# A recurrent chain's readouts: two kinds of products side by side, or one kind after the other

## The chip, the cores and the metric

The kernel runs on one core of one Trainium2 chip. The metric is device time in microseconds (us) from start to end of one execution; the median of several runs is quoted. PE is TensorE (products; PEld its weight loads), DVE is VectorE, ACT is ScalarE, POOL is GpSimd and SP the engine whose queue issues the DMAs.

## The reference

Two layers of a transformer block over 512 latent tokens (x) and 256 context tokens (ctx), width 1024. Each layer is an FFN, a mixing stage and a second FFN. The mixing stage has four mixers, one of which is RWKV-7, a linear recurrence run in both directions over the tokens, for four heads of 64 features:

```python
def wkv7_scan(r, decay, k, v, kk, b, s0, reverse):
    def step(s, inp):
        r_t, w_t, k_t, v_t, kk_t, b_t = inp
        sa = jnp.einsum('bhvk,bhk->bhv', s, kk_t)
        s = s * w_t[:, :, None, :] - sa[..., None] * b_t[:, :, None, :] + v_t[..., None] * k_t[:, :, None, :]
        return s, jnp.einsum('bhvk,bhk->bhv', s, r_t)     # state, readout
```

The second value of each step is the readout. The context's outputs aren't needed in the last layer, so that there the context's recurrence is run for its final state alone.

## The kernel before

Everything is laid out features first and written as generators of pieces of work. The program is a plain list of operations; a planner puts them into an order for each engine, from priorities and from the times that it works out for them, and adds the waits. PE runs its own list in that order.

The recurrence (`rwkv`) is computed in chunks of 64 tokens. A unit is two neighbouring chunks in one direction; the stages of successive units run beside each other: element-wise products and Gram matrices (`rw_elem`), inverses of small blocks by substitution on POOL (`rw_sub`, lines 1176 and 1177), inverses of whole chunks (`rw_lev`, lines 1203 to 1239), and the chain of states (`rw_chain`). Other work shares the engines: the first FFN of x while the context of layer 0 is in this stage, the second FFN of the context while x of layer 0 is, and attention and the RG-LRU mixer (lines 861 to 953) while x of layer 1 is. The FFNs' products, and all other products of large weights, stand on line 503.

In `rw_chain` each chunk has one bank of PSUM, the tile `pc`, in four parts of 128 columns: `pw`, `pu`, `ps` and `py`. The four heads lie as two pairs `p`; the two heads of a pair lie on partitions 0 to 63 and 64 to 127 (`H`). For each chunk there are

- line 1260: four products into `pw`, over 128 rows with 64 columns of weights; ACT copies them to `w` (line 1262)
- line 1266: four products into `pu`, over 64 rows with 64 columns of weights; ACT puts them into `uv` (line 1269)
- line 1275: four products into `ps`, over 128 rows: what the chunk adds to the state
- lines 1278 and 1279, only where the readout is needed: four products of the state over 128 rows into `py`, and four products of the chunk's own values over 64 rows that add to them
- line 1282: DVE makes the next state from `ps`, four operations; then line 1287 (ACT) or 1289 (DVE) brings `py` to `yt`

A product of float32 operands is two instructions on PE. All of `pc` is one bank, and the planner's waits keep the products into a bank and the reads of it in the order of the program, whichever parts they touch. The readout is needed for four context chunks of layer 0 in two directions (8), and for eight chunks of x in two directions in each layer (16 and 16): 40 chunks.

Of the kernel before, what the change touches and what calls it, by code (L numbers as in the profile page):

```python
# [15 lines left out]
D = 1024  # L16
# [12 lines left out]
# DRAM layout of eight [64, 64] matrices: the 16 x 16 blocks on all their diagonals lie one stride apart  # L29
MS = 4 * (BL * 64 + BL)  # L30

# columns of the packed shape constants
# [20 lines left out]
def shape_constants():  # L53
    import numpy as np

    c = np.zeros((128, C_N), np.float32)
    p = np.arange(128)
    c[p, C_ID + p] = 1.0
    s = p[:, None] % 64
    t = np.arange(64)[None, :]  # L60
    for d in range(2):
        strict = (s < t) if d == 0 else (s > t)
        incl = (s <= t) if d == 0 else (s >= t)
        for ty, m in enumerate((strict, incl)):
            o = C_MO + d * 128 + ty * 64
            c[:, o:o + 64] = m
        # mask for E[t, j]: row t in the later half, column j in the earlier half
        rows = (s // BL) % 2 == (1 if d == 0 else 0)
        cols = (t // BL) % 2 == (0 if d == 0 else 1)
        o = C_ML + d * 64  # L70
        c[:, o:o + 64] = rows & cols & (s // (2 * BL) == t // (2 * BL))
    c[:, C_I16:C_I16 + 256] = np.eye(16, dtype=np.float32).reshape(1, 256)
    c[:, C_RS:C_RS + 256] = np.arange(256)[None, :] % 64 != 0
    n = np.arange(NX, dtype=np.int32)
    inv = (np.float32(10000.0) ** (-np.arange(8, dtype=np.float32) / np.float32(8))).astype(np.float32)
    ang = np.stack([(n // 64).astype(np.float32)[:, None] * inv, (n % 64).astype(np.float32)[:, None] * inv], axis=1)
    ang = np.concatenate([ang, ang], axis=-1).reshape(NX, 32).astype(np.float32)
    for o in (0, 64):
        c[o:o + 32, C_RP:C_RP + 512] = np.cos(ang).astype(np.float32).T
        c[o + 32:o + 64, C_RP:C_RP + 512] = np.sin(ang).astype(np.float32).T  # L80
    return c


def arrange(inp):
    """the arrays as the launch takes them: tiles of weights contiguous, features first, small vectors as columns"""
# [38 lines left out]
def dhalf(t, h):  # L124
    """of eight [64, 64] matrices in DRAM every second one, from h on, as [64, 4, 64]"""
    return bass.AP(tensor=t.tensor, offset=t.offset + h * MS, ap=[[64, 64], [2 * MS, 4], [1, 64]])


def ddiag(t):
    """the 16 x 16 blocks on their diagonals as [32, 16, 16]"""  # L130
    return bass.AP(tensor=t.tensor, offset=t.offset, ap=[[MS // 4, 32], [64, BL], [1, BL]])


def upto(g, blocks):
    """the pieces of g up to the end of a number of its blocks"""
# [7 lines left out]
def some(g, n):  # L143
    """n pieces of g at a time"""
# [6 lines left out]
def merge(*gens):  # L151
    """the pieces of several generators in turn"""
# [5 lines left out]
def seg(t, s):  # L158
    """columns of t [p, 512]: s = 0, the middle half; 1, the outer quarters; None, all"""
# [3 lines left out]
def like(t, s):  # L163
    """t [p, 256] in the shape of such columns"""
# [15 lines left out]
class Net:  # L180
    def __init__(self, ctx, tc, ins, out):
# [4 lines left out]
        # the vector engine has much else to do while x goes through w_in: the low parts of its weights are GpSimd's  # L186
# [13 lines left out]
        # wb: a bank kept for the first stage of RWKV; piece: the last load of the modulations' weights  # L200
# [12 lines left out]
    def hold(self, name, side="left"):  # L213
        """a pool that stays until it is dropped"""
# [7 lines left out]
    def weights(self, side="left", raw=3, hi=2, lo=2):  # L222
        """the pool of the large weights"""
# [7 lines left out]
    def pM(self, h=None):  # L231
        """for the mixers: a bank for each of two of RWKV's stages (h), or for the others in turn"""
# [15 lines left out]
    # ---------------------------------------------------------------- setup  # L248
    def setup(self):
# [25 lines left out]
        # what the context leaves for the latent tokens of the same layer  # L275
# [34 lines left out]
    def params(self, l):  # L310
# [23 lines left out]
        # halves of the biases that go into tanh forms of sigmoids  # L334
# [9 lines left out]
        # softplus(-lambda)  # L344
# [15 lines left out]
    def ada(self, l):  # L360
        """mod[128, 72, 2]: feature chunk i * 8 + c of modulation i, for x and for ctx. Yields between pieces,
        True after each block of columns."""
# [39 lines left out]
    # ---------------------------------------------------------------- helpers  # L402
# [6 lines left out]
    def root(self, r, sums, n, eps):  # L409
        """r = 1 / sqrt(sums / n + eps)"""  # L410
# [7 lines left out]
    def rstd(self, tiles, N, groups, n, eps, tag="r", h=None):  # L418
        """1 / sqrt(sums / n + eps) of the sums of tiles over groups of partitions, on those partitions.
        The sums lie tokens first, a few columns, until they are spread"""  # L420
# [5 lines left out]
        # one accumulation: its start leaves none of the columns written, so that the first product for each replaces  # L426
# [11 lines left out]
    def meansq(self, pool, S, s, bank=None):  # L438
        """1 / rms of each token of a segment, on all partitions"""
# [16 lines left out]
    def norm(self, pool, hs, l, i, S, bank=None):  # L456
        """hs = modulated norm of the tokens, a segment at a time"""
# [15 lines left out]
    def loadw(self, src, new=None):  # L473
        """[128, nk, ncol] in DRAM -> exact high and low parts; new: where the tiles come from"""
# [22 lines left out]
    def gemm(self, W, c0, m, hs, N, ps=None, s=None, first=True, last=True):  # L497
        """PSUM tile [m, N] = W[:, :, c0:c0+m]^T hs, each operand a sum of two parts; s: only these columns"""
# [7 lines left out]
    def gemms(self, Ws, hs, S):  # L506
        """the products of several weights, a segment of the tokens after the other"""
# [16 lines left out]
    # ---------------------------------------------------------------- FFN  # L524
    @contextmanager
    def hidden(self, S, side="left"):
        """the tiles of an FFN: pools, input"""
# [7 lines left out]
    def ffn_groups(self, l, w13, w2, i, S, f, between=None, after=iter(())):  # L535
        """between: a generator of other pieces of work, one of which follows each tile of the hidden units;
        after: one that uses each segment of the result"""
# [31 lines left out]
    # ---------------------------------------------------------------- mixers  # L569
    def frame(self, S, a):  # L570
        """the mixers' inputs"""
# [14 lines left out]
    def mix(self, l, S, out, f=None, hs=None):  # L586
        """f: the tiles that hold the input, where nothing else wants the chip, so that the mixers run beside each other"""
# [49 lines left out]
    def others(self, l, S, out, pr, side, keep, first=iter(())):  # L637
        """first: the next of it comes before w_out; keep: the stack of pools that holds the tiles of w_out's rows"""
        if self.wide:
            # what is left of the modulations fills the tensor engine's gaps  # L640
# [45 lines left out]
    def wout(self, l, parts, S, s=None):  # L686
        """x += gate * (mixers' outputs @ their rows of w_out)"""
# [10 lines left out]
    def projector(self, l, S, hs, wp, nw=5, nr=2):  # L698
        """a tile of h @ w_in; work tiles of two kinds"""
# [5 lines left out]
    def winproj_c(self, l, S, hs, wp, out, pr):  # L705
# [6 lines left out]
        # C: token shift  # L712
# [18 lines left out]
        # normalised key  # L731
# [9 lines left out]
    def winproj(self, l, S, hs, wp, out, pr, nw=5, nr=2):  # L741
# [4 lines left out]
        # A: value times (1 + tanh(gate / 2)); the half is in the taps  # L746
# [9 lines left out]
        # D  # L756
# [30 lines left out]
        # B  # L787
# [11 lines left out]
        for c in range(2 if out else 0):  # L799
            ps = proj(768 + c * 128)  # L800
            # gelu, tanh form
# [10 lines left out]
    def rotcols(self, w):  # L812
        """columns 32..63 of w [128, k, 64] = the rotated partners of columns 0..31"""
# [5 lines left out]
    # ---- conv module  # L819
# [28 lines left out]
    # ---- RG-LRU  # L848
# [36 lines left out]
    # ---- MLA  # L885
    def mla(self, l, S, wp, yp, out, pr):
# [11 lines left out]
        # values, token-major  # L898
# [62 lines left out]
    # ---- RWKV-7  # L961
    def rwkv(self, l, S, wp, out, pr, deep):
        """stages of successive units run beside each other: element-wise products and Gram matrices; inverses of
        the blocks on the diagonals; inverses of the whole; chain of the states"""
# [34 lines left out]
    def rwkv_out(self, l, S, wp, pr, rw):  # L999
# [10 lines left out]
        for s in S.segs:  # L1010
            # the middle half is done while the last units are on their way, in the places of those that are through
# [31 lines left out]
    def slot(self, u, shape, tag, bufs):  # L1043
        """a tile in a ring of its own kind, each place of which lies where its first use puts it"""
        return u.wp.tile(shape, F32, tag=f"{tag}{u.i % bufs}", name=self.nm(tag), bufs=1)

    def rw_elem(self, u):
        """one direction of chunks b, b + 1 of all heads: 4 blocks q = 2 * pair + chunk, each with
        two heads on the diagonal"""
# [27 lines left out]
        # log of the decay products from a chunk's start, inclusive (cs) and exclusive (lw)  # L1077
# [17 lines left out]
        # channel-major: beta on the diagonal, kappa off it; alpha and rho on the diagonal, zeros off it  # L1095
# [37 lines left out]
        # token-major beta, kappa, scaled to the chunk's end  # L1133
# [20 lines left out]
    def gates(self, u, half):  # L1154
        """tanh forms of decay and rate of a direction's next four chunks"""
# [9 lines left out]
    def rw_sub(self, u):  # L1165
        """-(1 + L)^-1, transposed, of the 16 x 16 blocks on the diagonals by substitution, a block to a partition"""
# [25 lines left out]
    def rw_lev(self, u):  # L1192
        """the same of whole chunks by doubling blocks"""
# [3 lines left out]
        # values, token-major, off the diagonal (head 0 on partitions 64.., head 1 on partitions 0..)  # L1197
# [15 lines left out]
        def each(f):  # L1213
            """[128, 4, 64] in PSUM: f of each matrix's part and partitions"""
# [12 lines left out]
        # the last level has one block of 32 x 32 to fill, rows B, columns A  # L1227
# [14 lines left out]
    def rw_chain(self, u):  # L1242
# [11 lines left out]
        for c in order:  # L1254
# [19 lines left out]
            for p, H in PH if more else []:  # L1274
                nc.tensor.matmul(ps[H, p * 64:p * 64 + 64], bk[:, p * 2 + c, H], uv[:, p, H], start=True, stop=True)
            for p, H in PH if need_y else []:
                o, q = py[H, p * 64:p * 64 + 64], p * 2 + c
                nc.tensor.matmul(o, sv[:, p, H], wr[:, q, 1, H], start=True, stop=False)  # L1278
                nc.tensor.matmul(o, uv[H, p, H], lq[H, q, 1, :], start=False, stop=True)  # L1279
# [12 lines left out]
    # ---------------------------------------------------------------- end  # L1292
# [123 lines left out]
```

## Time and profile before

| | |
|---|---|
| median of 3 runs | 3439.17 us (3435.9 to 3445.69) |
| span of the profiled execution | 3440.0 us |
| PE busy | 3255.4 us (95% of the span) |
| DVE, ACT, POOL busy | 2020.9, 1389.9, 961.0 us |
| chunks with a readout | 40, in the stretches 713 to 846 us (8), 1408 to 1626 us (16), 2798 to 2970 us (16) |

The profiled execution took as long as the runs did. A product written as 128*64 in a row has 128 rows and 64 columns of the array; one written as 64*64 has 64 and 64. The chain that ended last is followed back from the last instruction: at each step to what released it, or to the instruction before it on its engine.

### The profile page before, as it was taken

Reading aid. Unit: us, or ns where it says so; the run is one execution under the profiler, and the core shown is the slowest. Engines: PE = TensorE matmul, PEld = TensorE weight load, DVE = VectorE, ACT = ScalarE, POOL = GpSimd, SP = SyncE. Lnnn points to the kernel's source line nnn. Section 1 sums busy time; section 2 is a strip of 40 time slices with the busy share of each in tenths; the row PEclk is TensorE's granted clock in tenths of the full one; section 3 lists DMA queues with packets and bytes.
Section 4 is the critical chain, followed back from the end, with each engine's and each line's share of the span. In section 5 each row is a group of like instructions: output and inputs, shape, how many; then the busy total and the mean of one; then the engine's idle time right before and its main releaser. Section 6 shows DMA issues by size and latency. Waiting matters only on the chain.

```text
span 3440.0 us, 52640 instructions
## 1 busy us (share of the span) xinstructions
PE 3255.4 (95%) x20670; PEld 2628.8 (76%) x20670; DVE 2020.9 (59%) x3437; ACT 1389.9 (40%) x2368; POOL 961.0 (28%) x1205
## 2 busy tenths in 40 slices
PE   7999999999898999899999999999999799889998
PEld 3797866777776789688987778888878557578887
DVE  4555853553797566875775544643348876463345
ACT  3444553233536443444555333422234334642223
POOL 0222301441331114772212521111124265021111
PEclk9999999999999999899999999999999899799999
DMA  9655545432223453343544324233333241033332
GB/s 333 201 183 182 167 148 159 132 86 75 83 72 113 125 168 118 89 119 116 155 136 127 92 85 129 76 108 93 98 98 94 79 108 30 25 113 102 98 95 83
DMA packets 203544, 403.43 MB, mean 117 GB/s; under 512 B 97569, under 2 KB 103201, under 8 KB 203297
## 3 DMA queue, kind: packets, MB, share of 16 engines
q1 hardware_dynamic: 203296, 400.07, 38.6%
q8 instruction: 163, 2.67, 0.3%
q14 instruction: 85, 0.69, 0.1%
HBM read 392.39 MB, written 7.61 MB: 116 GB/s over the span
## 4 chain that ended last, share of the span: by engine, by line
PE 77%; DVE 12%; ACT 3%; POOL 3%; issue 2%; DMA 2%; SPq 0%; DVEq 0%; ACTq 0%; POOLq 0%
PE pg L503 60%; DVE ac L829 3%; PE pt L503 2%; PE pg L380 2%; PE pc L1279 1%; PE pc L1278 1%; DVE wlo L494 1%; PE pm L380 1%; PE pm L1220 1%; PE pm L1119 1%; PE pc L953 1%; POOL bz L1177 1%; DVE nacc L448 1%; PE pt L936 1%; POOL bt L1176 1%
## 5 line engine op out<-in xcount | busy, mean ns | idle before, releaser
L503 PE MATMUL pg<-h,whi 128*128 128x256 f32 (+1 forms) x6128 | 1209.7, 345 | 20.1 <-ACT h L466 9.1
L503 PEld LDWEIGHTS pg<-h,whi 128*128 128x128 f32 x6128 | 974.7, 190 | 201.8 <-issue 29.4
L494 POOL TENSOR_TENSOR wlo<-raw,whi 128x1024 fp32r<-128x1024 f32 (+1 forms) x234 | 537.5, 2298 | 2015.8 <-ACT whi L490 1202.9
L490 ACT CAST whi<-raw 128x1024 fp32r<-128x1024 f32 (+1 forms) x621 | 607.2, 980 | 1079.7 <-PE pg L503 852.0
L494 DVE TENSOR_TENSOR wlo<-raw,whi 128x1024 fp32r<-128x1024 f32 (+1 forms) x387 | 450.3, 1165 | 410.8 <-ACT whi L490 191.5
L503 PE MATMUL pg<-h,wlo 128*128 128x256 f32 (+1 forms) x3064 | 630.4, 344 | 6.7 <-DVE wlo L494 4.6
L503 PE MATMUL pg<-hid,whi 128*128 128x256 f32 (+1 forms) x2688 | 548.2, 340 | 20.1 <-DVE hid L517 5.8
L503 PEld LDWEIGHTS pg<-h,wlo 128*128 128x128 f32 x3064 | 490.6, 190 | 91.0 <-issue 17.1
L503 PEld LDWEIGHTS pg<-hid,whi 128*128 128x128 f32 x2688 | 424.7, 192 | 93.7 <-issue 12.8
L503 PE MATMUL pg<-hid,wlo 128*128 128x256 f32 (+1 forms) x1344 | 289.0, 334 | 1.1 <-DVE wlo L494 0.8
L522 DVE SCALAR_TENSOR_TENSOR x<-pg,msc,x 128x512 f32<-128x512 f32 (+1 forms) x232 | 155.2, 674 | 190.3 <-PE pg L503 189.2
L503 PEld LDWEIGHTS pg<-hid,wlo 128*128 128x128 f32 x1344 | 217.9, 192 | 26.2 <-DVE wlo L494 1.2
L517 DVE TENSOR_TENSOR hid<-ft,hid 128x512 fp32r<-128x512 f32 (+1 forms) x154 | 135.2, 878 | 61.6 <-ACT hid L516 61.2
L516 ACT CAST hid<-ft 128x512 fp32r<-128x512 f32 (+1 forms) x154 | 81.3, 528 | 218.2 <-DVE ft L552 216.7
L552 DVE SCALAR_TENSOR_TENSOR ft<-pg,ft 128x512 f32<-128x512 f32 (+1 forms) x152 | 86.7, 571 | 131.1 <-PE pg L503 130.6
L829 DVE SCALAR_TENSOR_TENSOR ac<-z,dw,ac 128x512 f32<-128x512 f32 (+1 forms) x180 | 142.2, 831 | 1.3
L551 DVE SCALAR_TENSOR_TENSOR ft<-ft,pg 128x512 f32<-128x512 f32 (+1 forms) x152 | 86.1, 567 | 89.4 <-ACT ft L550 89.0
L1177 POOL TENSOR_TENSOR bz<-bz,bt 32x14 f32<-32x14 f32 (+6 forms) x336 | 110.7, 329 | 24.0
L1176 POOL TENSOR_TENSOR bt<-bu,bz 32x14 f32<-32x14 f32 (+6 forms) x336 | 108.0, 321 | 22.7
L550 ACT ACTIVATE ft<-pg 128x512 f32<-128x512 f32 (+1 forms) x152 | 76.7, 504 | 72.0 <-PE pg L503 71.6
L466 ACT ACTIVATE h<-nt,mod 128x256 fp32r<-128x256 f32 x136 | 64.8, 503 | 75.9 <-DVE nt L465 75.6
L522 DVE SCALAR_TENSOR_TENSOR ctx<-pg,msc,ctx 128x256 f32<-128x256 f32 x144 | 68.1, 479 | 45.3 <-PE pg L503 43.2
(356 smaller groups left out, 3490.5 us busy)
## 6 DMA issues: line engine op xcount, KB each, us to landing
raw<-in_ffn_w_dram SPq DMA_DIRECT2D x456, 512.0 KB, 3.6
aw<-in_ada_w_dram SPq DMA_DIRECT2D x72, 512.0 KB, 5.1
raw<-in_ada_w_dram SPq DMA_DIRECT2D x72, 512.0 KB, 4.0
raw<-in_w_in_dram SPq DMA_DIRECT2D x65, 512.0 KB, 3.6
raw<-in_w_out_dram SPq DMA_DIRECT2D x56, 256.0 KB, 2.7
raw<-in_ffn_w_dram SPq DMA_DIRECT2D x40, 256.0 KB, 2.9
dl<-lq SPq DMA_DIRECT2D x48, 64.0 KB, 2.2
xt<-dz SPq DMA_DIRECT2D x48, 64.0 KB, 2.4
```

What stands on the lines that cost most here:

```text
L380: nc.tensor.matmul(pa[j * 32:(j + 1) * 32, :], self.cT[:, k, :], w[:, (j % 2) * 512:(j % 2) * 512 + 512], start=(k == 0), stop=(k == 7))
L490: nc.scalar.copy(out=hi[:, 0:n], in_=raw[:, 0:n])
L494: eng.tensor_tensor(out=lo[:, 0:n], in0=raw[:, 0:n], in1=hi[:, 0:n].bitcast(F32), op=ALU.subtract)
L503: self.nc.tensor.matmul(seg(ps[0:m, 0:N], s), W[w][:, k, c0:c0 + m], seg(hs[k][:, q, 0:N], s), start=(first and i == 0), stop=(last and i ...
L516: nc.scalar.copy(out=dst[:, 0, 0:N], in_=src[:, 0:N])
L517: nc.vector.tensor_tensor(out=dst[:, 1, 0:N], in0=src[:, 0:N], in1=dst[:, 0, 0:N].bitcast(F32), op=ALU.subtract)
L522: self.nc.vector.scalar_tensor_tensor(out=x, in0=seg(ps[:, 0:S.n], s), scalar=gate(m, S.i), in1=x, op0=ALU.mult, op1=ALU.add)
L551: nc.vector.scalar_tensor_tensor(out=t, in0=t, scalar=1.0, in1=pg[:, 0:N], op0=ALU.add, op1=ALU.mult)
L552: nc.vector.scalar_tensor_tensor(out=t, in0=pu[:, 0:N], scalar=0.5, in1=t, op0=ALU.mult, op1=ALU.mult)
L829: V.scalar_tensor_tensor(out=ac, in0=z, scalar=w, in1=ac, op0=ALU.mult, op1=ALU.add)
L1176: nc.gpsimd.tensor_tensor(out=tt, in0=u.u[:, I, k:k + 1].to_broadcast([32, n, m]), in1=z[:, k:k + 1, J].to_broadcast([32, n, m]), op=ALU.mult)
L1177: nc.gpsimd.tensor_tensor(out=z[:, I, J], in0=z[:, I, J], in1=tt, op=ALU.subtract)
```

## The change

For each chunk with a readout the four products over 128 rows are issued first, and then the four over 64 rows that add to them; before, each was followed by its own. The number of products, their operands and their places in PSUM stay. Of the start flags only those of the first pair of heads are left: a start marks the columns of its partitions in the bank as not written, so that the first product into each replaces what is there, and one start for each half of the partitions, ahead of all eight, does that for both pairs. The stop flag stands on the last pair's adding products. The lines keep their numbers: after the change line 1277 is the product over 128 rows and line 1279 the one over 64.

```diff
             for p, H in PH if need_y else []:
-                o, q = py[H, p * 64:p * 64 + 64], p * 2 + c
-                nc.tensor.matmul(o, sv[:, p, H], wr[:, q, 1, H], start=True, stop=False)
-                nc.tensor.matmul(o, uv[H, p, H], lq[H, q, 1, :], start=False, stop=True)
+                nc.tensor.matmul(py[H, p * 64:p * 64 + 64], sv[:, p, H], wr[:, p * 2 + c, 1, H], start=(p == 0), stop=False)
+            for p, H in PH if need_y else []:
+                nc.tensor.matmul(py[H, p * 64:p * 64 + 64], uv[H, p, H], lq[H, p * 2 + c, 1, :], start=False, stop=(p == 1))
```

The rest of the diff empties lines that held comments.

## Rows read from the trace of the kernel before

**Rows 1.** The page: span; part 1 (busy time, share, instructions).

```profile
span 3440.0 us, 52640 instructions
PE 3255.4 (95%) x20670; PEld 2628.8 (76%) x20670; DVE 2020.9 (59%) x3437; ACT 1389.9 (40%) x2368; POOL 961.0 (28%) x1205
```

**Rows 2.** Chain that ended last, by line: 713:846, 1408:1626, 2798:2970 us.

```profile
by line: PE pg L503 72.3%; PE pc L1279 6.1%; PE pc L1278 5.3%; PE pm L1220 3.8%; PE pc L1275 2.3%; PE pm L1234 2.0%; PE pc L1260 2.0%; PE pc L1266 2.0%; PE pm L1119 1.6%; PE pm L1203 0.9%; PE pm L1138 0.9%; PE pm L1067 0.8%
...
by line: PE pg L503 42.9%; PE pc L1279 7.2%; PE pc L1278 6.5%; POOL bz L1177 4.1%; PE pm L1220 4.0%; POOL bt L1176 3.6%; PE pm L1119 3.6%; issue 2.5%; PE pc L1275 2.4%; PE pm L1234 2.3%; PE pc L1266 2.1%; PE pc L1260 1.9%; PE pm L1022 1.6%;
...
by line: PE pg L953 11.6%; PE pc L1279 9.4%; PE pc L1278 8.3%; PE pg L861 5.5%; PE pt L936 5.5%; PE pg L950 4.7%; PE pm L1220 4.6%; issue 3.6%; PE pm L1119 3.1%; PE pc L1275 2.9%; ACT p L943 2.6%; PE pt L938 2.3%; PE pg L919 2.1%; PE pm L12
```

**Rows 3.** Busy time of each engine in those stretches and within one readout.

```profile
core 0: us, PE busy (x) PEld busy (x) DVE busy (x) ACT busy (x) POOL busy (x), PEclk, DMA share, GB/s
713.00:846.00 133.00, 133.00 (x1006) 103.93 (x1005) 61.11 (x112) 40.10 (x82) 38.55 (x75) 1.00 0.28 79
1408.00:1626.00 218.00, 208.75 (x2227) 181.33 (x2225) 149.58 (x312) 98.68 (x216) 128.03 (x243) 0.95 0.39 106
2798.00:2970.00 172.00, 160.15 (x1704) 112.65 (x1704) 100.65 (x248) 82.81 (x214) 73.46 (x202) 0.95 0.11 20
...
1419.50:1422.60 3.10, 3.10 (x20) 2.20 (x16) 1.92 (x2) 0.07 (x1) 0.23 (x1) 0.50 0.00 0
```

**Rows 4.** Chain in order of time: start, us, what; 700:860 us.

```profile
725.90 0.38 PE pc L1266 x8
726.28 0.47 PE pm L1220 x16
...
768.11 0.38 PE pc L1275 x8
768.49 0.11 PE pc L1278 x2
768.60 0.25 PE pc L1279 x2
768.86 0.26 PE pc L1278 x2
...
770.14 0.25 PE pc L1279 x2
...
770.77 4.98 PE pg L503 x21
...
794.51 0.38 PE pc L1260 x8
794.89 0.61 PE pm L1220 x16
```

**Rows 5.** The same, 1418:1424, 2941:2947 and 2962:2967 us.

```profile
1419.68 0.21 PE pc L1278 x2
...
1422.30 0.40 PE pc L1279 x2
...
2941.83 0.74 PE pc L1266 x8
...
2944.59 0.28 PE pc L1278 x2
2944.87 0.40 PE pc L1279 x2
...
2962.85 0.41 PE pc L1278 x2
```

**Rows 6.** Instructions on tile pc, ns min/median/max; who waited (us, times).

```profile
L1278 PEld LDWEIGHTS pc<-wr,su x320: 132/136/232, 713.5 to 2965.3; 128*64 128x64 f32 x160
L1278 PE MATMUL pc<-wr,su x320: 222/222/367, 713.6 to 2965.4; 128*64 128x64 f32 x160
L1279 PE MATMUL pc<-lq,uv x320: 218/267/366, 713.8 to 2965.8; 64*64 64x64 f32 x160
...
  DVE su L1282: 34.9, 20
```

## The prediction

> **What bounds the kernel now.** I read the page first: PE is busy for 95% of a span of 3440.0 us [rows 1]. That alone says little, so I went to the chain that ended last, cut to the three stretches in which readouts are issued [rows 2]. The reader is to see that lines 1278 and 1279, sixteen short instructions a chunk, hold 11.4% of the first stretch (133 us, 15.2 us), 13.7% of the second (218 us, 29.9 us) and 17.7% of the third (172 us, 30.4 us): 75.5 us in all on the path that sets the end. In the first stretch every group of that path is PE; in the second POOL's lines 1177 and 1176 have 7.7% of it, and in the third ACT's line 943 has a place. The busy times agree [rows 3]: PE is busy for all of the first stretch, for 208.75 of 218 us in the second and for 160.15 of 172 us in the third, so it idles for 0, 9.25 and 11.85 us. No other engine comes near: DVE is at most 149.58 of 218.
>
> Then I read the pieces of the chain in order of time [rows 4]. One readout begins at 768.49 and has eight pieces of two instructions each; the first takes 0.11 us, the others 0.25 or 0.26, until 770.40: 1.9 us. Beside it stand the same kinds of products without alternation. Line 1275 (128*64, as line 1278 is) has eight instructions in 0.38 us; line 1266 (64*64, as line 1279 is) also eight in 0.38. Sixteen of line 1220 (64*64) take 0.47 us where they follow line 1266, which has the same tile, and 0.61 us where they follow line 1260, which has the other.
>
> **What a change of tile costs.** Line 1220 gives the pitch, 0.47 / 16 = 0.03 us for an instruction, and the change of tile, 0.61 - 0.47 = 0.14 us. Line 1275 gives the same: 0.38 - 8 * 0.03 = 0.14. In the readout a piece of two instructions takes 0.26: the change, and two instructions that have no partner in the other half of the array to run beside. So the seven changes inside a readout, and the pairs that they tear apart, are its cost; both directions cost alike (0.26 for line 1278 after line 1279, 0.25 the other way), so it isn't that an adding product waits for the one that it adds to, since a step into line 1278 has no such product before it.
>
> **The change, part by part.** Nothing is removed or added but the order and two start flags; the operand shapes stay, no DMA, no copy and no wait is added, and all sixteen instructions still need what line 1269 made before the last of them can run.
>
> The four products over 128 rows follow line 1275, which has their tile: eight at the pitch, 8 * 0.03 = 0.24 us, without a change. The four adding products are one change and eight instructions, as line 1266: 0.38 us. After: 0.62 us. Before: 0.11 + 7 * 0.255 = 1.90. Gain: 1.28 us a chunk at full clock. What follows stays as it is: the next tile after line 1279 is the same as now.
>
> Some readouts lie at the lower of the clock's two levels: in the one at 1419.68 the granted clock is 0.50 of 2.4 GHz, so 1.2 GHz, against 1.00 in the whole first stretch [rows 3]. There all pieces take 0.40 but the first, 0.21 [rows 5]: 3.0 us; the one at 2962.85 has some 0.4 for each too, 3.2 us. Line 1266 takes 0.74 at that level, and eight more at twice the pitch 0.48: 1.2 us after, so 1.8 to 2.0 gained; I take 1.9 for each. The readout at 2943.74 falls from the upper to the lower level in its middle (0.28, then 0.40): about 2.3 us; after the change it would have ended within 0.62 us, before that fall: 1.7.
>
> The sum on PE: 8 * 1.28 = 10.2 us in the first stretch, 15 * 1.28 + 1.9 = 21.1 in the second, 14 * 1.28 + 1.9 + 1.7 = 21.5 in the third: 52.8 us.
>
> **What of it lies on the path.** In the first stretch all 15.2 us of eight readouts are on the chain and PE never idles: 10.2 us count. In the second 29.9 us are on the chain of 15 * 1.9 + 3.0 = 31.5 (95%): 20.0. In the third 30.4 of 14 * 1.9 + 3.2 + 2.3 = 32.1 (95%): 20.4. That is 50.6 us. Against it stands work of other engines that will be late next: POOL's substitutions in the second stretch, ACT's and DVE's share of attention in the third. What they can take I price by PE's idle share now, 9.25 / 218 = 4% and 11.85 / 172 = 7%: 0.8 and 1.4 us. Left: 48.4 us. The bounds: all 52.8 carried, 3387; below, half of the second and third stretch lost, 10.2 + 20.2 = 30.4 us, 3410. I take the upper part, since DVE's state update itself waits for line 1279 (34.9 us over 20 times [rows 6]), so the chain of states is shortened with PE's work and not only beside it. The profiled execution has the time of the runs (3440.0 against a median of 3439.17). 3440 - 48 = 3392 us.
>
> **Two rules weighed.** The rows of line 1266 show eight instructions that alternate between the two halves of the rows, into one bank, at the pitch of 0.03 us after the change of tile [rows 4]. The Trainium skill (TensorEngine Tiling (Array Packing), Restrictions and Gotchas) says that different row tiles can't reach one PSUM bank at once; by it the adding products would run one by one. The trace doesn't agree, since line 1266 has that case.
>
> The rows of line 1275 show eight instructions over all 128 rows, with alternating halves of the columns, in 0.38 us, though a load of line 1278's kind is 136 ns and its product 222 ns [rows 4, 6]: loads are hidden. The Trainium skill (TensorE: Matmul & The Clock Gate, Part 3) has a weight load overlap a running product only where the row group differs, and here it never differs. Again the trace doesn't agree.
>
> **The rivals.**
>
> Half absorbed: the second and third stretch become bound by POOL and ACT. For: POOL's 7.7% of the chain [rows 2]. Against: POOL is busy for only 128.03 of 218 us [rows 3]. It gives 3410, as worked out; 14%.
>
> No gain that shows: 0.3%, some 10 us, is what a measurement of this kernel can tell from no change. Either the readout's cost isn't the change of tile, so that each short product keeps its 0.13 us, or all but the first stretch is lost: 3430 or more. Against: lines 1266 and 1275 [rows 4]. 7%.
>
> One by one: if the adding products don't overlap in one bank, they take another 0.24 us a chunk, 9.6 us in 40: 3401; 4%.
>
> Loads not hidden: eight instructions over 128 rows would cost 8 * (0.136 + 0.222) = 2.9 us; with 0.38 that is 3.2 against 1.9, 40 * 1.3 = 52 us more: 3492. It decides once loads in a row of equal tiles are exposed by more than 1.28 / 8 = 0.16 us. Line 1275 denies it; 1%.
>
> Planner: the four products over 128 rows don't need `uv`, so the planner could put a block of FFN products between them and the adding ones. Such a block is 4.98 us [rows 4], and the state update waits behind it: 4.98 - 1.28 = 3.7 us more of chain for a chunk. In the first two stretches, 24 chunks, that is 89 us where the chain of states outlasts the work that fills it, against 53 gained: 3476. It makes the kernel slower by 0.3% from 17 such chunks on ((53 + 10) / 3.7). For: no data tie the two halves. Against: in the chunk of [rows 4] line 1278 follows line 1275 directly though it needs no `uv` either; 4%.
>
> **How the numbers follow.** The forecast, nearly all carried, has 70%: 3383 (52.8 and a few us of waits that vanish with a shorter chain) to 3402 (10 us less than forecast). Half absorbed and one by one lie on the same side: faster 0.70 + 0.14 + 0.04 = 0.88, no change 0.07, slower 0.04 + 0.01 = 0.05. The range of 3383 to 3416 holds the forecast's own, one by one, and most of half absorbed, and leaves the rest out.
>
> **What would show it.** In the trace after, in each chunk: eight instructions of line 1277 right behind line 1275, then one step of some 0.14 us, then eight of line 1279; from the first to the end 0.62 us in the chain, and the two lines at 0.7 to 0.8% of the whole chain together. The first stretch should be 10 us shorter, the second and third some 19 each. PE's idle time in the second and third stretch shows what was absorbed. The forecast is wrong if line 1279 is apart from line 1277 by other products, if the adding products still take 0.26 us a pair, or if POOL, ACT or DVE end PE's idle time for more than some 15 us beyond the 21.1 of now.

## The result, and the profile after

The changed kernel takes 3396.64 us (median of 4 runs, 3394.18 to 3401.43), the kernel before 3437.53 us (4 runs, 3434.33 to 3445.69). The ratio is 0.9886, with a 95% interval of 0.9873 to 0.9899: 41 us faster, where 48 were forecast (3392, in a range of 3383 to 3416). The profiled execution's span is 3399.7 us.

One correction to what stands above: the lines do move, by two. In the changed kernel the four products over 128 rows stand on line 1279 and the four adding ones on line 1281.

The page after, to be read beside [rows 1]:

```profile
span 3399.7 us, 52623 instructions
PE 3207.9 (94%) x20670; PEld 2598.6 (76%) x20670; DVE 2027.2 (60%) x3437; ACT 1383.2 (41%) x2364; POOL 961.9 (28%) x1205
```

PE is busy for 47.5 us less, and the span is 40.3 us shorter: PE idles for some 7 us more.

The pieces of the chain in order of time (start, us, what), of one chunk at the upper level of the clock and one at the lower, for the chunks of [rows 4] and [rows 5]:

```profile
764.53 0.38 PE pc L1275 x8
764.91 0.23 PE pc L1279 x8
765.14 0.38 PE pc L1281 x8
...
1409.81 0.43 PE pc L1279 x8
1410.23 0.62 PE pc L1281 x8
```

The eight products over 128 rows go on at 0.23 us, and the eight adding ones take 0.38 with the change of tile in front: 0.61 us at the upper level (0.62 was forecast, 1.9 was before) and 1.05 at the lower. Of the 40 chunks 34 take 0.61 us, one 0.67, and the one at the lower level 1.05. The last chunk of x in each direction of each layer has no line 1275 in front, since no state is needed after it, so that its first eight products begin with a change of tile too: three of these four chunks take 0.76 us (2.05 before), and the last, at 2926.67, takes 1.89, at the lower level and with a wait of 0.56 us for ACT's line 1269.

The chain that ended last, by line, in the three stretches of the changed kernel, for [rows 2]:

```profile
by line: PE pg L503 64.0%; issue 4.2%; POOL bt L1176 3.4%; POOL bz L1177 3.2%; PE pm L1220 2.7%; PE pc L1275 1.9%; PE pc L1266 1.9%; PE pc L1281 1.9%; DMA dl<-lq 1.8%; PE pm L1119 1.8%; PE pc L1260 1.6%; DMA bu<-dl 1.5%; PE pm L1234 1.5%; P
...
by line: PE pg L503 39.9%; POOL bt L1176 5.7%; issue 4.9%; PE pm L1119 4.3%; POOL bz L1177 4.2%; PE pm L1220 3.7%; PE pc L1281 2.3%; PE pm L1234 2.0%; PE pc L1266 2.0%; PE pc L1275 1.9%; PE pc L1260 1.8%; PE pm L1022 1.7%; PE pc L1279 1.6%;
...
by line: PE pg L953 11.0%; PE pt L936 6.1%; issue 5.7%; PE pg L950 5.5%; PE pm L1220 4.0%; PE pg L919 3.7%; PE pm L1119 3.5%; ACT p L943 3.3%; PE pt L938 2.6%; DMA xx<-dz 2.5%; PE pm L1022 2.4%; DVE svf L1284 1.9%; PE pm L1234 1.9%; DVE su 
```

Lines 1279 and 1281 together are below 4% of the second stretch (13.7% before), and in the first and third line 1279 has dropped out of what the view lists. What has moved up is POOL's substitution (lines 1176 and 1177: from 7.7% to 9.9% of the second stretch, from none to 6.6% of the first) and time that is put down to issue. In the first stretch this costs nothing yet: PE idles for 0.26 of 117.68 us there, as the next table shows.

Busy time of each engine from the first readout to the end of the last in each stretch, after:

```profile
core 0: us, PE busy (x) PEld busy (x) DVE busy (x) ACT busy (x) POOL busy (x), PEclk, DMA share, GB/s
713.53:831.21 117.68, 117.42 (x982) 92.61 (x978) 58.06 (x106) 38.04 (x80) 38.52 (x75) 1.00 0.30 84
1399.08:1607.80 208.72, 191.99 (x2221) 170.61 (x2217) 154.15 (x311) 97.52 (x215) 127.77 (x242) 0.93 0.40 110
2780.18:2927.99 147.81, 135.27 (x1690) 96.30 (x1687) 97.54 (x243) 79.72 (x211) 73.69 (x205) 0.97 0.13 23
```

and the same of the kernel before:

```profile
713.56:841.26 127.70, 127.70 (x982) 99.74 (x978) 58.45 (x106) 38.42 (x80) 38.39 (x75) 1.00 0.27 78
1408.95:1626.06 217.11, 207.86 (x2221) 180.80 (x2217) 148.63 (x311) 97.73 (x215) 127.08 (x242) 0.95 0.39 107
2798.82:2966.08 167.26, 155.49 (x1688) 109.90 (x1684) 98.03 (x243) 82.00 (x213) 72.70 (x200) 0.96 0.11 20
```

The first column is the time of the stretch: 127.70 to 117.68 us (10.0 less, 10.2 forecast), 217.11 to 208.72 (8.4 less, 19.2 forecast), 167.26 to 147.81 (19.5 less, 19.0 forecast). So two stretches came out as worked out, and the second gave less than half. There PE's busy time fell by 15.9 us, and its idle time (time less busy) rose from 9.3 to 16.7 us.

Both parts fell short. Added up over its 16 chunks, from the end of the product ahead to the end of the last, the readouts of the second stretch went from 31.9 to 10.5 us: 21.4 less, where 21.1 were forecast. But PE's other work there, the same instructions as before, took 5.5 us more. More of it ran at the lower level of the clock (before in one piece, after in four, whose sum is shown; the granted clock is 0.50 in each):

```profile
1415.53:1436.01 20.48, 15.40 (x70) 10.68 (x72) 18.07 (x42) 9.39 (x22) 12.73 (x26) 0.50 0.21 48
...
sum 27.31, PE 23.93 PEld 19.99 DVE 20.54 ACT 12.73 POOL 18.36; mean PE 5.98 PEld 5.00 DVE 5.13 ACT 3.18 POOL 4.59
```

Line 503 has 849 instructions in the stretch, 8 of them in such a piece before and 46 after; one adds 0.24 us there and 0.13 at the upper level. By these numbers line 503 alone makes some 4 of the 5.5 us, an estimate.

### The profile page after: what moved, and what is told of

Read it like the earlier page. It is cut to its first block, busy times and chain, and to the rows that moved or that the text cites. A ratio compares the mean times of both kernels' runs of the same rounds, so it can differ in the third digit from the quotient of the medians.

```text
span 3399.7 us, 52623 instructions
## 1 busy us (share of the span) xinstructions
PE 3207.9 (94%) x20670; PEld 2598.6 (76%) x20670; DVE 2027.2 (60%) x3437; ACT 1383.2 (41%) x2364; POOL 961.9 (28%) x1205
## 4 chain that ended last, share of the span: by engine, by line
PE 76%; DVE 13%; ACT 3%; issue 3%; DMA 2%; POOL 2%; SPq 0%; DVEq 0%; ACTq 0%; POOLq 0%
PE pg L503 60%; DVE ac L829 3%; PE pg L380 2%; PE pt L503 2%; DVE wlo L494 1%; PE pm L1119 1%; PE pm L380 1%; PE pt L936 1%; PE pc L953 1%; ACT whi L490 1%; DVE nacc L448 1%; PE pm L503 1%; POOL bt L1176 1%; PE pm L1220 1%; POOL bz L1177 1%
```

## The experiments

The planner made another order for the changed kernel from the second stretch on, on all engines; up to there nothing but the readouts differs. So the first question was whether this order, which nobody asked for, took the 10 us (theory P), or whether the grouping itself brings PE sooner to results that DVE and POOL do not have ready (theory S; the first expectations call it theory A).

| run | time, us | kernel before, same chip | ratio (95% interval) |
|---|---|---|---|
| grouped, order of before | 3399.48 | 3435.79 | 0.9895 (0.9877 to 0.9912) |
| alternating, order of after | 3436.16 | 3435.79 | 1.0003 (0.9991 to 1.0015) |
| by twos | 3406.73 | 3435.79 | 0.9917 (0.9900 to 0.9934) |
| second stretch only | 3427.90 | 3435.79 | 0.9977 (0.9966 to 0.9989) |
| third stretch only | 3414.09 | 3436.50 | 0.9932 (0.9918 to 0.9947) |
| low parts off POOL (not in the second stretch), after | 3390.24 | 3436.97 | 0.9862 (0.9850 to 0.9875) |
| low parts off POOL (not in the second stretch), before | 3431.75 | 3436.97 | 0.9984 (0.9976 to 0.9993) |
| two operations on ACT, after | 3398.71 | 3436.97 | 0.9889 (0.9875 to 0.9903) |
| two operations on ACT, before | 3436.56 | 3436.97 | 1.0001 (0.9992 to 1.0009) |
| light, alternating | 3420.28 | 3436.50 | 0.9956 (0.9941 to 0.9972) |
| light, grouped | 3382.63 | 3436.50 | 0.9843 (0.9828 to 0.9857) |

**Order and grouping apart.** The kernel before is planned as it was, with the start flags of the change, and afterwards, in the finished list, the eight products of each chunk change places among their own eight places:

```python
pairs = READOUTS[g:g + 4]                 # a chunk's four (product, adding product)
places = sorted(at[name(i)] for p in pairs for i in p)
want = [ins[at[name(p[0])]] for p in pairs] + [ins[at[name(p[1])]] for p in pairs]
for n, i in zip(places, want):
    ins[n] = i
```

> The planner's order is that of the kernel before, instruction for instruction on every engine; only within each of the 40 chunks are the eight products rearranged, as in the change. Theory P (the changed kernel lost some 10 us because the planner made another order for the second stretch): nearly all of the 53 us comes through, 3437.5 - 49 = 3388 us, ratio 0.986, and the second stretch gets some 19 us shorter instead of 8. Theory A (what PE gains there is taken by POOL, DVE and ACT, whatever the order): as the changed kernel, 3397 us, ratio 0.988, second stretch 8 us shorter.

Its counterpart takes the changed kernel's order and lets the products alternate again (`want = [ins[at[name(i)]] for p in pairs for i in p]`).

> The planner's order is that of the changed kernel; within each chunk the products alternate again as before. Theory P: the new order costs some 10 us by itself, so slower than the kernel before: 3447 us, ratio 1.003. Theory A: as the kernel before, 3437 us, ratio 1.000.

Theory P falls twice. With the old order grouping gains 36 us, no more than with the new one, and the new order with alternating products is as fast as the kernel before. The order costs nothing that can be seen; the loss in the second stretch comes with the grouping itself. Busy time in the three stretches of the grouped kernel with the old order:

```profile
716.43:833.99 117.56, 117.39 (x982) 92.62 (x978) 58.23 (x106) 38.08 (x80) 38.66 (x75) 1.00 0.29 84
1399.77:1606.88 207.11, 189.24 (x2221) 167.93 (x2217) 149.98 (x311) 97.84 (x215) 127.08 (x242) 0.95 0.39 110
2778.42:2925.45 147.03, 131.78 (x1689) 94.19 (x1686) 97.78 (x243) 80.16 (x210) 72.45 (x199) 0.98 0.13 23
```

The pattern is that of the changed kernel: 10.1, 10.0 and 20.2 us less. In the second stretch the mean granted clock is 0.95 as before, so the clock has a small part in the loss there: the readouts take 21.0 us less, PE's other work 2.4 more, and PE's idle time rises from 9.3 to 17.9.

Since this kernel has the same list of instructions on every engine as the kernel before, the two traces can be laid side by side. PE's waits in the second stretch (for whom, us in total, times, longest), grouped:

```profile
PE pg L503 <- POOL wlo L494: 2.9, 1, 2.9
PE pg L503 <- DVE h L467: 2.1, 1, 2.1
PE pm L1138 <- DVE wr L1126: 2.0, 3, 0.9
...
PE pm L1119 <- DVE wr L1126: 1.4, 2, 1.1
...
PE pm L1119 <- POOL bt L1176: 0.8, 1, 0.8
PE pm L1138 <- POOL bx L1134: 0.8, 2, 0.4
...
PE pm L1119 <- POOL bz L1177: 0.6, 1, 0.6
```

and in the kernel before:

```profile
PE pg L503 <- DVE h L467: 1.7, 1, 1.7
...
PE pm L1119 <- DVE wr L1126: 1.1, 1, 1.1
PE pm L1138 <- POOL bx L1134: 0.9, 1, 0.9
PE pm L1138 <- DVE wr L1126: 0.9, 1, 0.9
...
PE pg L503 <- POOL wlo L494: 0.3, 1, 0.3
```

Short waits, each below 1.2 us, at the places where PE takes up what DVE or POOL made for the next unit (lines 1119 and 1138), and ahead of the FFN's products one of 2.9 us for a low part of weights (0.3 before) and one of 2.1 for DVE's line 467 (1.7 before). In all, waits for POOL went from 1.2 to 5.1 us, for DVE from 5.0 to 8.3, for ACT from 3.1 to 4.4. How one of them comes about is seen in PE's rows and, below the dots, DVE's (start, us, engine, line, operation, count, idle before). Grouped:

```profile
1492.79 1.10 PE L1119 MATMUL pm<-wr,bx 128*128 128x256 f32 x4 [1.14 <-DVE wr L1126]
...
1494.45 0.40 PE L1278 MATMUL pc<-wr,su 128*64 128x64 f32 x8
1494.79 0.45 PE L1279 MATMUL pc<-lq,uv 64*64 64x64 f32 x8
...
1499.24 0.63 PE L1138 MATMUL pm<-cst,bx 128*128 128x128 f32 x4 [0.71 <-DVE wr L1126]
...
1495.09 2.11 DVE L494 TENSOR_TENSOR wlo<-raw,whi 128x1024 fp32r<-128x1024 f32 x1 [2.44 <-ACT whi L490]
...
1498.24 0.85 DVE L1126 TENSOR_TENSOR wr<-pm,cst 64x256 f32<-64x256 f32 x2
```

Before, the same instructions:

```profile
1506.01 1.03 PE L1119 MATMUL pm<-wr,bx 128*128 128x256 f32 x4
...
1507.60 0.28 PE L1278 MATMUL pc<-wr,su 128*64 128x64 f32 x2
1507.81 0.32 PE L1279 MATMUL pc<-lq,uv 64*64 64x64 f32 x2
...
1512.81 0.60 PE L1138 MATMUL pm<-cst,bx 128*128 128x128 f32 x4
...
1507.95 2.11 DVE L494 TENSOR_TENSOR wlo<-raw,whi 128x1024 fp32r<-128x1024 f32 x1 [2.45 <-ACT whi L490]
...
1511.10 0.85 DVE L1126 TENSOR_TENSOR wr<-pm,cst 64x256 f32<-64x256 f32 x2
```

Line 1138 needs the bank that DVE's masked products (line 1126) read, and in DVE's list those stand behind a split of weights (line 494) that takes 2.1 us. In the kernel before, line 1119 starts at 1506.01, the split at 1507.95, the last pair of masked products at 1511.10, and PE comes to line 1138 at 1512.81 without a wait: 1.71 us behind the start of that pair. Grouped, they start at 1492.79, 1495.09 and 1498.24, and PE, with the readout behind it sooner, stands for 0.71 us and starts line 1138 at 1499.24, 1.00 us behind the pair's start. Without a wait it would have been there at 1498.53, so the start of line 1138 had 0.71 us of slack before (1.71 less 1.00). Without its wait PE's way from line 1119 to line 1138 is 1.06 us shorter than before (6.80 less 5.74), so that the shorter readout makes 0.35 us of the wait; the other 0.36 come from DVE, whose pair starts 5.45 us behind line 1119 instead of 5.09. The readout had been cover for a chain on DVE.

**Fewer changes of tile, but not one.** The order of before; `want` takes the products in twos: two over 128 rows, the two that add to them, and again.

> The order of the kernel before; in each chunk two products over 128 rows, the two that add to them, two over 128 rows, two that add: three changes of tile instead of seven (or one). If each change costs the same, a readout takes 0.12 + 3 * 0.26 = 0.90 us instead of 1.90 and 0.62: 40 us less PE work in all, 38 after the loss in waits, 3400 us, ratio 0.989. If the cost lay in an adding product that waits for the product that it adds to (two instructions apart here), each of the four adding products would still wait and no more than half of the gain would show: 3412 us or more, ratio 0.993.

The chain's pieces of one chunk:

```profile
761.80 0.38 PE pc L1275 x8
762.18 0.12 PE pc L1278 x4
762.30 0.26 PE pc L1279 x4
762.56 0.27 PE pc L1278 x4
762.83 0.26 PE pc L1279 x4
```

0.91 us, against 0.90 expected: a change and four instructions take 0.26 to 0.27, as a change and two did. Without a change the four take 0.12 and the two took 0.11 (the first piece here and in [rows 4]), so the change of tile is 0.14 to 0.15 us in both, and two instructions without a partner in the other half take nearly as long as four that have one. The time, 3406.73, is 29 us less, where 38 were expected. The rival, an adding product that waits for its own, gave 3412 or more; the interval of the time (3401 to 3413) just touches that, but the pieces decide: they last as long into line 1278 as into line 1279, so it falls. Here too the second stretch holds back: against twos, grouping saves another 4.7 us of its readouts, but the stretch went from 208.65 to 207.11 us only, since PE's idle time rose from 14.1 to 17.9.

**One stretch at a time.** The exchange is made in the chunks of one stretch only (`for g in range(8 * 4, 24 * 4, 4)`, and from 24 to 40).

> The order of the kernel before; the products are rearranged only in the 16 chunks of the second stretch (x of layer 0). Theory P: 21.1 us of PE work less, 20 on the path: 3437.5 - 19 = 3418 us, ratio 0.9945. Theory A: 8 us, 3429 us, ratio 0.9975.

> The order of the kernel before; the products are rearranged only in the 16 chunks of the third stretch (x of layer 1). Work on PE falls by 21.5 us. With the waits that the full grouping shows there (3.5 us more idle time): 18 to 20 us off, 3418, ratio 0.9945. If the third stretch gained only because the earlier ones had moved it, it would be well under 10.

7.9 us (interval 4 to 12) and 22.4 us (18 to 28). They and the remainder of the whole, some 10 us for the first stretch (40.9 - 7.9 - 22.4 = 10.6), fit the stretches of the profile within these intervals. The second stretch loses its gain also when nothing ahead of it has changed: PE's idle time there is 18.2 us. The 22.4 us are more than the readouts can give (21.4 us less in that stretch's profile); PE's other work took 2.3 us less there too, with a mean granted clock of 0.98 in place of 0.96.

**POOL relieved.** If POOL is what PE waits for, relieving it should let more through. The first relief gives low parts of the FFN's weights to DVE alone, and was meant for the second stretch:

```diff
+                    self.off_pool = l == 0 and i == 2 and S.i == 1
...
-        eng = nc.gpsimd if self.spl % 3 == 0 or self.pool_splits else nc.vector
+        eng = nc.gpsimd if (self.spl % 3 == 0 or self.pool_splits) and not self.off_pool else nc.vector
```

> The changed kernel, and in the second stretch the low parts of the context FFN's weights are made by DVE alone (before: every third by POOL, 12 of 2.37 us). Theory S (the second stretch is now bound by what POOL and DVE deliver to PE's next units, which come late by a fraction of a microsecond each): POOL has 28 us less to do in that stretch, DVE some 14 us more; the waits for POOL's low part (2.9 us) and some of those for its substitutions (2.2 us) go: 3 to 5 us off, 3392 to 3394. Rival C (the missing gain is lost to the clock and not to POOL): no change, 3397. DVE may take it back: 3397 or more too, with PE's waits on POOL gone and waits on DVE in their place.

> The same move of the low parts to DVE in the kernel before, as its control. Theory S: the alternating readouts hide POOL's lateness, so at most 1 us: 3437. Rival C: no change, 3437.

The edit missed the stretch. Its condition names the context's second FFN of layer 0, whose last groups end as the readouts of x begin; what runs beside those readouts is the context's first FFN of layer 1, the next in the program (the description of the kernel before has the second FFN for this whole stage). POOL's splits of weights in the second stretch, in the changed kernel and with the edit:

```profile
L494 POOL TENSOR_TENSOR wlo<-raw,whi 128x1024 fp32r<-128x1024 f32 x12 | 28.8, 2404 | 45.5 <-ACT whi L490 32.4 <-PE pg L503 13.1
...
L494 POOL TENSOR_TENSOR wlo<-raw,whi 128x1024 fp32r<-128x1024 f32 x12 | 28.8, 2399 | 40.0 <-ACT whi L490 24.4 <-PE pg L503 11.2 <-issue 4.5
```

Twelve of 2.4 us in both. The 23 splits that POOL lost lie ahead of it (52 to 29 between the first and the second stretch). So this pair, and both its expectations, say nothing on theory S. The kernel is faster by 6.4 us than the changed kernel's median, but the control gains 5.2 us as well: grouping gains 41.5 us on top of the move, not to be told from 41. What the move gives comes ahead of the second stretch, where the time from the last readout of the first is 11.7 us shorter, and 12.6 in the control; a part of it is lost again further on. Of the kernels that leave nothing out it has the lowest median.

The other relief moves two of POOL's operations of each unit to ACT, in the second stretch:

```diff
+            if self.batch:
+                nc.scalar.activation(out=kd[:, p, :], in_=ta0[:, p, :], func=AF.Identity, scale=pr["hka"][:, p:p + 1], bias=pr["ka1"][:, p:p + 1])
+            else:
...
+        for q in range(4 if self.batch else 0):
+            nc.scalar.activation(out=bx[:, q, :], in_=bx[:, q, :], func=AF.Identity, scale=u.pc[:, q:q + 1])
```

> The changed kernel, and in the second stretch two of POOL's operations of each unit go to ACT: the rate's affine form (line 1091, two of 1.0 us) and the scaling to the chunk's end (line 1134, one of 1.04 us); some 24 us less of POOL's 128, while ACT is at 98 of 212. These stand ahead of the transposes on which PE waits. Theory S: PE's waits on POOL (some 5 us in that stretch) mostly go and units start earlier: 4 to 8 us off, 3389 to 3393. Rival C: no change, 3397.

> The same two operations on ACT in the kernel before, as the control. Theory S: PE's own work hides POOL there (PE waits 0.3 us for POOL's low part and 0.9 for line 1134 in the stretch): at most 2 us, 3436. Rival C: 3437.

Neither kernel is faster for it. POOL is busy for 109 us in the stretch instead of 128, but PE's waits for POOL hardly change: 5.5 us, 4.2 of them for the substitution (line 1177 of the changed kernel), against 5.9 without the relief. So the amount of POOL's work that this relief takes away isn't what makes it late; whether another part is, it doesn't show. The rows show what happened. Control, second stretch and what lies between it and the third:

```profile
1398.67:1608.24 209.57, 203.51 (x2159) 175.73 (x2155) 142.60 (x301) 105.23 (x240) 110.05 (x218) 0.94 0.38 103
1608.24:2792.71 1184.47, 1136.18 (x6429) 930.32 (x6430) 691.72 (x1086) 453.39 (x729) 326.91 (x364) 0.98 0.35 108
```

and with the change:

```profile
1394.78:1586.83 192.05, 174.79 (x2121) 153.86 (x2117) 136.83 (x298) 102.45 (x237) 108.95 (x218) 0.96 0.38 105
1586.83:2775.06 1188.23, 1140.24 (x6469) 935.92 (x6469) 694.30 (x1090) 456.77 (x735) 325.10 (x360) 0.98 0.35 109
```

The second stretch now gets 17.5 us shorter by the grouping, nearly what was forecast, yet its idle time still grows, from 6.1 to 17.3 us, and what follows gets 3.8 us longer: the recurrence ends sooner and leaves more of the FFN's products (6469 instructions after it instead of 6429) to be done behind it. A shorter stretch isn't yet a gain.

**POOL and DVE relieved by leaving work out.** Both kernels leave out POOL's substitution loop and half of DVE's masked products in the second stretch, and have the same order on every engine.

```diff
-        for k in (range(BL - 2, 0, -1) if d == 0 else range(1, BL - 1)):
+        for k in [] if self.batch else (range(BL - 2, 0, -1) if d == 0 else range(1, BL - 1)):
...
-                for h in range(2):
+                for h in range(0 if self.batch and rows else 2):
```

> The control of the next: the kernel before, alternating, with work left out in the second stretch only: POOL's substitution loop (lines 1176 and 1177, 28 operations a unit) and the four of DVE's eight masked products of a unit that fill the off-diagonal part (line 1126), so that the recurrence's values there are not the reference's. POOL has some 60 us less to do there and DVE some 14. PE's work is the same. Both theories: a few us faster than the kernel before, since PE idles 9.3 us in that stretch: 3425 to 3437.

> The same with the readouts grouped, and with the same order of every engine otherwise. Theory S (in the second stretch PE now waits for suppliers that have too much to do): with POOL and DVE relieved, grouping adds no more than 3 us to PE's idle time there (8.6 in the full kernel), the second stretch gets 16 to 18 us shorter, and the whole gain against its control is 42 to 46 us. Theory L (PE waits for round trips PE to another engine to PE of one unit, whose length doesn't come from load, and which the longer readout used to cover): idle grows by some 8 us as before, and the gain is 36 to 40.

The second stretch, alternating:

```profile
1395.47:1579.21 183.74, 175.06 (x1980) 149.58 (x1976) 123.66 (x274) 89.22 (x205) 57.62 (x59) 0.97 0.37 100
```

and grouped:

```profile
1384.49:1555.72 171.23, 158.80 (x1980) 138.61 (x1976) 124.13 (x274) 89.15 (x205) 57.40 (x59) 0.94 0.40 106
```

Idle time grows from 8.7 to 12.4 us, by 3.7 instead of 8.6. That is a little over the 3 us that theory S allowed and far from the 8 of theory L. PE waits for POOL in neither of the two, where grouping had brought 3.9 us more of such waits in the old order; so it is likely that about half of the waits come from the load on POOL and DVE. It is not shown beyond that: these two kernels have a plan of their own, and the pair with low parts off POOL, which has POOL's full load in the stretch, shows a rise of 4.8 us (11.1 to 15.9).

The stretch gets 12.5 us shorter, not 16 to 18, and the clock makes the difference: the readouts take 20.6 us less, PE's other work 4.4 more, with a granted clock of 0.94 in place of 0.97. The whole gain is 37.7 us, below the 42 to 46 that theory S asked for; in the profile the third stretch, where nothing was left out, fell short too (163.80 to 148.65 us, 15.2 less instead of 19.5). So these two runs don't settle which theory is right for the total.

## Why the prediction was right, point by point

The price of a change of tile held. The step from 1.90 to 0.62 us a chunk was measured as 1.9 to 0.61, from rows of lines 1266, 1275 and 1220 that stood in the trace before. By twos gave the third point, 0.91. The Trainium skill (TensorEngine Tiling (Array Packing), Tiling Modes) says that a change of tiling mode drains the engine; the trace agrees as far as it can, with 0.14 us for a change at the upper level of the clock.

The two rules that spoke against the change are answered by the readouts themselves: eight adding products in alternating halves of the rows, into one bank, take 0.38 us, so one by one falls; eight over 128 rows take 0.23 us with loads of 0.14 us each in the same row group, so loads not hidden falls. The planner put nothing between the two kinds of products in any chunk, so that rival falls too.

Three readings were off, with little in the sum. Four of the 40 chunks don't follow line 1275, but that holds before and after, and their gain is the same (2.05 to 0.76 us). The 0.74 us of line 1266 at 2941.83 were not at the lower level: the granted clock is 1.00 until 2944.70, and the eight came spread out behind a wait. At the lower level eight products take 0.43 us, and 0.62 with the change in front, so a readout there takes 1.05 and not 1.2. And of the 34.9 us for which DVE's state update waited, 30.5 are for line 1279; after the change its successor, line 1281, has 11.0, in line with the shorter chain of states that the prediction counted on.

What of it lies on the path was right for the first stretch (10.0 of 10.2 us) and the third (19.5 of 19.0; 22.4 when it is changed alone), and wrong in size for the second (8.4 of 19.2). There the changes, in us, are

| second stretch | changed kernel | grouped, order of before | light pair |
|---|---|---|---|
| readouts on PE | -21.4 | -21.0 | -20.6 |
| PE's other work | +5.5 | +2.4 | +4.4 |
| PE's idle time | +7.5 | +8.6 | +3.7 |
| the stretch | -8.4 | -10.0 | -12.5 |

The first row was right. The term that failed is the 0.8 us for work of other engines that will be late next. I had priced it by PE's idle share, 4%; it measured 7.5 us in the changed kernel and 8.6 with the old order. The idle time before says how often PE is late now; the price of a shorter readout is what is left of the slack of the results that PE takes up behind it, and in the second stretch that slack was small in several places (0.71 us in the one followed above): low parts of weights from POOL, masked products from DVE behind a split, POOL's substitutions. This is the rival half absorbed, but in one stretch alone, so that the time lies between it and the forecast. It was shown that the waits come with the grouping and not with the planner's order. That the load on POOL and DVE makes about half of them is argued from one pair of runs. How much of the total would come back with that load gone stays open: one of the two reliefs that leave nothing out missed the stretch, and the other left the waits for POOL as they were.

The second row is a term that the sum doesn't have: I had counted the lower level of the clock for the readouts alone, and not where it falls on PE's other work once the order in time shifts. An estimate, from what the same line's products take at the upper level in the same run, puts 5.0 of the 5.5 us down to it, all of the 4.4, and 0.8 of the 2.4. In the third stretch PE's other work took 1.4 us more in the changed kernel, which this doesn't explain (0.97 against 0.96), and 2.3 less when that stretch is changed alone (0.98). So a part of what a single stretch gains or loses is where the low level happens to lie.

## What to carry to other kernels

Products of different tile shapes that alternate cost a change of tile each, here 0.14 us, as much as five instructions that follow one of their own shape (0.23 us for eight), and the pairing of the two halves besides; look in the trace for short products whose pieces take equal time in both directions, and sort them by shape where the sums allow it. Before counting such a gain in full, measure for each result that the engine takes up next how long it has been ready: a slack smaller than the gain is what the gain ends at, and the idle time of now doesn't show it. A planner's new order looks like the culprit when the traces differ everywhere; exchanging the instructions in the finished list, in both directions, takes two runs and can clear it, as here. And before a relief is believed to have had no effect, look in its trace whether the work is gone from the stretch that was meant.

## What was not expected of the hardware

The low level of the clock came and went in other places in each run, although PE's products were the same: in the second stretch its mean was 0.95 before, 0.93 after, 0.95 grouped with the old order, 0.97 and 0.94 in the light pair. What sets where it falls was not tested.
